# Conv tile 7's taps on TensorE for both chunks in two phases, and one more block of the first down projection by seven products

## The chip, the cores and the metric

The kernel runs on one core of one Trainium2 chip. The metric is the device time of one execution in microseconds, from the first to the last instruction with what lies around them. Besides the executions that are only timed, one execution was recorded by the hardware profiler; every view of the trace shown here is of that one.

A core has TensorE (PE in the profile, its weight loads as PEld), VectorE (DVE), ScalarE (ACT), GpSimd (POOL) and SyncE (SP, which here only issues DMAs). Each engine has its own instruction queue and works it off in order.

## The reference

Two layers over one sequence of 1024 tokens with 1024 channels, all in float32. Layer 0's mixer is the Conformer module, layer 1's a pooling mixer; each is followed by a SwiGLU feed-forward with F = 2816 hidden channels (22 F tiles of 128). Every sub-layer is RMS-normed, shifted, scaled and gated by a conditioning vector.

```python
# layer 0's mixer
u = h @ w1 + b1
a, g = jnp.split(u, 2, axis=-1)
u = a * jax.nn.sigmoid(g)
u = causal_depthwise_conv(u, w_dw, width=31) + b_dw     # one filter of 31 taps per channel
u = jax.nn.silu(layer_norm(u, ln_g, ln_b))
y = u @ w2 + b2
# layer 1's mixer: in four channel groups, trailing mean over 2, 4, 8, 16 tokens minus the token, then a linear map
# both layers' feed-forward
y = (silu(h @ w_gate) * (h @ w_up)) @ w_down
```

## The kernel before

**Layout.** Channels lie on the 128 partitions (8 tiles of channels), tokens along the free axis, in two chunks A and B of 512 tokens. TensorE's order is written out by hand: the program is a list of units, each a group of matmuls with the weights that it takes (`run_units`, up to five weight tiles `w` ahead, `W_BUFS`). Everything else is emitted between the units by `pace`, which steps background tasks as far as a running estimate of each engine's clock allows (`AHEAD`, `PRICES`, `DELAY`); the framework then orders the other engines' instructions.

**Products.** A product of two float32 tiles is three matmuls of 128x128 by 128x512 in the fp32r type (`products`): weight and activation are each split into a high part (ScalarE's cast) and a low part (value minus high part, VectorE as a rule), and high times high, high times low and low times high are summed in one PSUM bank.

**Conv taps.** The 31 taps of a channel tile are, for most tiles, scaled adds: VectorE adds `u * w` into a PSUM accumulator `ca`, ScalarE makes `pr = u * w` and GpSimd adds it into `pa`; class `Taps` hands each tap to whichever is free. Two tiles have taps on TensorE, where a tap is a matmul with a diagonal 128x128 weight (`PE_TAPS`, `pe_taps`): 15 taps of tile 6 and all 31 of tile 7, both for chunk A only. In chunk B all eight tiles go through VectorE and GpSimd. After chunk A's taps comes its layer norm (`layer_norm_silu`, task `ln_a`) beside three units of chunk B's `conv_in`, then `conv_out`. Chunk B's taps and layer norm (`ln_b`) run beside the first part of the feed-forward, and `conv_b` waits for it.

**Feed-forward of layer 0.** Gate and up projections are taken for F tiles in pairs `fp`. For `fp` 0 to 7 the even F tile of chunk A is computed classically and kept (`heads`), in two rounds of four, each followed by `down` of those four F tiles over all eight output tiles: 96 matmuls a round. The other gate and up products are done jointly for A and B by a scheme of seven products in place of eight (`all_joint`). The down projection is then finished in `first_down`. It has blocks `q` of two pairs (`q` = 5 has one), and each block has eight half products: odd or even F tile, chunk A or B, lower or upper half of the output channels; each is 24 matmuls (12 for `q` = 5). Blocks below `BEGINS[0] // 2` are classical, the others take seven products p1 to p7 with combined weights (s1 to s4) and combined activations (`kinds`, made in `paired` and kept in DRAM). Before, `q` = 0 to 3 are classical and `q` = 4, 5 (F tiles 16 to 21) go by seven. The order is: a and b (chunk A's odd tiles, both halves), p2, p1, p6, p7, p4, p5, p3, then c, d, e, f (chunk B). The weight sums s1, s2, s3 are made on VectorE in `weights`, from blocks a11, a21, a22 loaded ahead.

**Around it.** After p1 the pooling mixer of chunk A starts as a task on VectorE; its second half of x is whole only when p4 has ended; its output products (`pool_out`, tiles `mx`) come in `pool_end`, after e. `norm_a` of layer 1 then runs beside f.

Of the kernel before, what the change touches and what calls it, by code (L numbers as in the profile page):

```python
# [16 lines left out]
P = 128  # L17
D = 1024
# [35 lines left out]
DIAGS = 8  # L54
LOAD = {"load": 4.0, "both": 9.5, "slow": 6.0, "next": 4.0, "dots": 4.0}
# [5 lines left out]
BEGINS = (8, 0)  # L61
# [10 lines left out]
DELAY = {"stats": 2.75, "spread": 3.0, "soon": 0.5, "settled": 3.0, "later": 5.0, "root": 3.4}  # L72
# [4 lines left out]
for _name, _w in (  # L77
    ("ada_b", DEPTH * 6 * KT), ("norm_mix_g", DEPTH * KT), ("norm_ffn_g", DEPTH * KT),
    ("conv_b1", 2 * KT), ("conv_bdw", KT), ("conv_ln_g", KT), ("conv_ln_b", KT), ("conv_b2", KT),
    ("c", KT), ("pool_ls", KT), ("final_g", KT), ("conv_wdw", CW * KT),  # L80
):
    _COLS[_name] = _n
    _n += _w
# [18 lines left out]
def tap_groups(p):  # L102

    n = PE_TAPS[p]

    todo = list(range(CW - 1, -1, -1) if n == CW else range(CW - 3, CW - 3 - 2 * n, -2))
# [27 lines left out]
def trunk(ctx, tc, xT, c, vec, ada, adan, w1f, w1, wdg, w2, wgu, wdn, wds, wpl, out):  # L134
# [597 lines left out]
    def conv_u(ch, p):  # L732
        u = st["u", ch.i, p] = wslot(ch, "u", p)
        if ch.i == 0:
# [5 lines left out]
    def conv_glu(ch, p, ba, bg, own=False):  # L740
# [5 lines left out]
        if ch.i == 0 and PE_TAPS.get(p) == CW:  # L746

            V_.scalar_tensor_tensor(ba, ba, V("conv_b1", p), sg, op0=ADD, op1=MUL)
            pair = wpair(B, "us", F32R)
            hi, lo = st["us", p] = [pair[:, i, : ch.width] for i in range(2)]  # L750
            for part in (hi, lo):
                G_.memset(part[:, HALO - 2 : HALO].bitcast(F32), 0.0)
            S_.copy(hi[:, HALO:], ba)
            V_.tensor_tensor(lo[:, HALO:], ba, hi[:, HALO:].bitcast(F32), op=SUB)
            S_.copy(uhalo[:, p, :], ba[:, ch.n - HALO :])
            return
# [34 lines left out]

    def split_u(p):
# [6 lines left out]
    def pe_taps(p):  # L799
# [4 lines left out]
        for i, js in enumerate(groups):  # L804
            def emit(take, i=i, js=js):
# [3 lines left out]
                for q, j in enumerate(js):  # L809
                    full = PE_TAPS[p] == CW  # L810
                    o = (CW - 1 - j) // 2 * 2 if full else CW - 3 - j
                    c = j + o if full else 0
                    products(b[:, o:], wt, q, [v[:, c : c + A.n - o] for v in st["us", p]], j == groups[0][0], j == groups[-1][-1])
                    if q % 4 == 3:
                        pace()
                if i == len(groups) - 1:
                    if full:
                        S_.activation(st["u", 0, p][:, HALO:], b, AF.Identity, bias=V("conv_bdw", p))
                        st["taps", 0][p] = True
                    else:  # L820
                        T["taps", 0, p].other = b
# [86 lines left out]
    def layer_norm_silu(ch):  # L908
# [17 lines left out]
        yield "soon" if ch.i else "stats"  # L926
# [51 lines left out]
    def conv_out(ch, squares, then=None):  # L978
# [17 lines left out]
        for ds in [(0, 1) if ch.i else (0,), *(() if ch.i else ((1,),)), *((d,) for d in range(2, KT))]:  # L996
# [475 lines left out]
    def down(ch, l, fs, then=()):  # L1472

        def half(d0, wd):
            def kept(take, give):
                gs = [st["g", ch.i, f] for f in fs]
                last = len(gs) - 1
                todo = [range(4)] if not d0 else [range(2), range(2, 4)]
                for ds in todo:
                    bs = {d: bank("dn") for d in ds}  # L1480
                    for i, g in enumerate(gs):
# [6 lines left out]
                        if ds is todo[-1] and d0:  # L1488
# [164 lines left out]
    def first_down(l, after):  # L1653

        SIDE = {"odd": 0, "even": 1}
        duo, one = BY_SEVEN[l]
        todo, raw, banks, ready, counts = [], {duo: {}, one: {}}, {}, {}, [0, 0]
# [10 lines left out]
        def fetched_raw(name, b):  # L1668
            for q in (one, duo):
# [3 lines left out]
        def first_blocks():  # L1673
            wide = [block("u0", "raw", F32).rearrange("p a b -> p (a b)") for _ in range(2)]
            both = block("u0", "raw", F32)
            raw[duo].update(a11=wide[0], a22=wide[1])
            raw[one].update(a11=both[:, 0], a22=both[:, 1])
            fetched_raw("a11", 0)
            fetched_raw("a22", 3)

        def second_blocks():
            a21, a21_one = (block("h1", "a21", F32).rearrange("p a b -> p (a b)") for _ in range(2))
            raw[duo]["a21"], raw[one]["a21"] = a21, a21_one[:, : duo_width(one) * 512]
# [573 lines left out]
```

## Time and profile before

| | |
|---|---|
| median of 3 runs | 1677.97 us (1677.6 to 1678.09) |
| the profiled execution | 1675.66 us |
| its span, first to last instruction | 1673.9 us |
| mean granted TensorE clock | 0.998 |
| matmuls | 7550 |
| PE busy | 1651.8 us, 99% |
| DVE busy | 1310.0 us, 78% |
| ACT busy | 804.1 us, 48% |
| POOL busy | 487.4 us, 29% |

The profiled execution was 2.3 us shorter than the median of the timed ones, and 1.76 us of it lie outside the span. In rows of the profile `out<-in` gives the tiles that an instruction writes and reads, `xN` how many instructions a row joins, and what stands in brackets the idle time before it and who ended that. All kernel calls go through helpers, so nearly all compute rows have line L128 or L151; tiles tell them apart. Matmuls are pipelined, so the time that one takes in a stream is the spacing of starts, not the duration of one: the chain of waits shows it, since it counts each from the end of the one before.

### The profile page before, as it was taken

To read this page: it belongs to the slowest core of one execution; us is meant where nothing else is said; L and a number is where in the kernel's file an instruction comes from. 1 tells how busy PE (TensorE), PEld (TensorE's weight loads), DVE (VectorE), ACT (ScalarE), POOL (GpSimd) and SP (SyncE) were. 2 spreads that over 40 slices of the span, in tenths; PEclk is the share of its full clock that TensorE was granted. 3 is DMA by queue.
4 is the path that set the end of the run, shared out by engine and by line. 5 is a ranking of instruction groups with operands and counts; after the bars stand their busy time and mean duration, and the time that the engine had idled before them with its cause. 6 is when DMAs were issued, how large, how long until landed. Compare 5 with 4: busy or idle time off the path is not lost.

```text
span 1673.9 us, 21194 instructions
## 1 busy us (share of the span) xinstructions
PE 1651.8 (99%) x7550; PEld 1351.2 (81%) x7550; DVE 1310.0 (78%) x1867; ACT 804.1 (48%) x1090; POOL 487.4 (29%) x567
## 2 busy tenths in 40 slices
PE   7999999999999999999999999999999999999997
PEld 5777878787888888888888888888888888888887
DVE  8889899799759888888678957848777766658657
ACT  3669696867546332332234436637322222244354
POOL 3587777796002111221100502101111111000013
PEclk9999999999999999999999999999999999999999
DMA  8958997828776888886965959866777776686664
GB/s 301 295 176 228 225 236 205 226 78 241 229 234 168 278 264 287 282 272 206 400 231 164 285 155 283 247 211 199 189 225 222 220 227 183 207 273 207 192 170 126
DMA packets 117180, 378.60 MB, mean 226 GB/s; under 512 B 12369, under 2 KB 14545, under 8 KB 117074
## 3 DMA queue, kind: packets, MB, share of 16 engines
q1 hardware_dynamic: 79664, 245.63, 41.6%
q0 software_dynamic: 36832, 131.09, 32.5%
q8 instruction: 59, 0.97, 0.2%
q10 hardware_dynamic: 578, 0.53, 0.1%
q14 instruction: 47, 0.39, 0.1%
HBM read 310.61 MB, written 62.39 MB: 223 GB/s over the span
## 4 chain that ended last, share of the span: by engine, by line
PE 88%; POOL 3%; DVE 2%; DMA 2%; issue 2%; ACT 2%; DVEq 0%; SPq 0%; POOLq 0%; ACTq 0%
PE a L151 24%; PE dn L151 23%; PE e L151 14%; PE p L151 10%; PE y L151 6%; POOL pa L128 3%; PE first L151 3%; PE g L151 2%; PE tap L151 2%; DMA adaw<-in_adan_dram 1%; DMA s<-in_wds_dram 1%; PE ada L151 1%; ACT w L128 1%; DMA w<-in_wgu_dram 1%; PE var L151 1%
## 5 line engine op out<-in xcount | busy, mean ns | idle before, releaser
L128 ACT CAST w<-raw 128x1024 fp32r<-128x1024 f32 (+1 forms) x247 | 254.6, 1033 | 305.5 <-PE dn L151 56.9
L128 DVE TENSOR_TENSOR w<-raw,w 128x1024 fp32r<-128x1024 f32 (+1 forms) x173 | 209.3, 1214 | 62.2 <-ACT w L128 61.9
L151 PE MATMUL a<-n,w 128*128 128x512 f32 x1056 | 246.8, 389 | 0.2
L151 PE MATMUL p<-h,w 128*128 128x512 f32 x1056 | 243.7, 390 | 1.2 <-DMA w<-in_wgu_dram 1.0
L128 POOL TENSOR_TENSOR pa<-pa,pr 128x512 f32<-128x512 f32 x159 | 225.3, 1500 | 29.0 <-ACT pr L128 23.7
L151 PEld LDWEIGHTS p<-h,w 128*128 128x128 f32 x1056 | 197.3, 188 | 43.7 <-DMA w<-in_wgu_dram 1.4
L151 PEld LDWEIGHTS a<-n,w 128*128 128x128 f32 x1056 | 198.0, 188 | 42.2 <-DVE r L128 1.1
L151 PE MATMUL dn<-hi,w 128*128 128x512 f32 (+1 forms) x768 | 226.2, 377 | 0.4 <-DVE w L128 0.4
L151 PE MATMUL dn<-g,w 128*128 128x512 f32 x864 | 199.1, 390 | 0.2 <-DVE x L128 0.2
L151 PEld LDWEIGHTS dn<-g,w 128*128 128x128 f32 x864 | 161.7, 188 | 34.7 <-DVE x L128 0.6
L128 DVE SCALAR_TENSOR_TENSOR ca<-u,vecs,ca 128x512 f32<-128x512 f32 x246 | 170.6, 747 | 0.5
L151 PEld LDWEIGHTS dn<-hi,w 128*128 128x128 f32 x768 | 141.2, 188 | 27.0 <-DVE w L128 0.9
L151 PE MATMUL dn<-lo,w 128*128 128x512 f32 (+1 forms) x384 | 144.3, 376 | 0.0
L151 PE MATMUL a<-t,w 128*128 128x512 f32 x528 | 123.3, 389 | 0.0
L151 PE MATMUL e<-t,w 128*128 128x512 f32 x528 | 123.3, 389 | 0.0
L151 PE MATMUL e<-b,w 128*128 128x512 f32 x528 | 123.3, 389 | 0.0
L128 ACT ACTIVATE pr<-u,vecs 128x512 f32<-128x512 f32 x159 | 108.4, 717 | 25.0 <-POOL pa L128 19.7
L151 PEld LDWEIGHTS a<-t,w 128*128 128x128 f32 x528 | 99.1, 188 | 20.7
L151 PEld LDWEIGHTS e<-t,w 128*128 128x128 f32 x528 | 99.1, 188 | 20.6
L151 PEld LDWEIGHTS e<-b,w 128*128 128x128 f32 x528 | 99.1, 188 | 20.6
L1191 POOL DMA_DIRECT2D raw<-in_wgu_dram x41 | 36.5, 889 | 271.5 <-DVE r L128 104.2
L128 ACT CAST hi<-op 128x1024 fp32r<-128x1024 f32 (+1 forms) x52 | 48.5, 935 | 87.1 <-PE dn L151 77.2
(191 smaller groups left out, 2449.4 us busy)
## 6 DMA issues: line engine op xcount, KB each, us to landing
raw<-in_wgu_dram SPq DMA_DIRECT2D x132, 512.0 KB, 4.7
raw<-in_wds_dram SPq DMA_DIRECT2D x48, 512.0 KB, 6.0
adaw<-in_ada_dram POOLq DMA_DIRECT2D x48, 512.0 KB, 6.8
kinds<-k POOLq DMA_DIRECT2D x42, 512.0 KB, 7.7
raw<-in_wgu_dram POOLq DMA_DIRECT2D x41, 512.0 KB, 7.3
raw<-in_w_dram SPq DMA_DIRECT2D x36, 512.0 KB, 6.6
op<-kinds SPq DMA_DIRECT2D x36, 512.0 KB, 4.8
adaw<-in_adan_dram SPq DMA_DIRECT2D x32, 512.0 KB, 5.5
```

The costliest lines, as they stand in the source:

```text
L128: self.last = self.order(getattr(self.eng, name)(out, *args, **kw))
L151: last_mm[0] = nc.tensor.matmul(out, lhsT, rhs, start=start, stop=stop, skip_group_check=more).ins.name
L1191: d = order(nc.gpsimd.dma_start(w[i], wgu[l, fp, src], accum_op=ADD))
```

## The change

1. **Tile 7's taps.** Both chunks of tile 7 are now done on TensorE, as two groups of 64 channels. `halves` writes the gated value so that partitions 0 to 63 hold the even tokens and 64 to 127 the odd tokens of 64 channels; a dense 128x128 weight then does two taps for both phases at once, and a group takes 16 steps (`NM`) over 512 columns, which cover 1024 tokens. That is 2 groups x 16 steps x 3 = 96 matmuls (`pe_halves`) in place of 31 taps x 3 = 93 of 482 to 512 columns. VectorE does four gated multiplies of 64 x 256 a chunk in place of one of 128 x 512, and ScalarE writes the result back in four pieces of 64 x 256 a group. Tile 7 of chunk B no longer goes through VectorE and GpSimd.
2. **Block q = 3 by seven products.** `BEGINS` goes from 8 to 6, so F tiles 12 to 21 (`q` = 3, 4, 5) go by seven. In `heads` the second round's `down` leaves out F tiles 12 and 14 for the upper half; for the lower half they stand for that block's p2. c and d now cover `q` = 0, 1, and e and f only `q` = 2; `pool_end(A)` comes after d.
3. **Weight sums on GpSimd.** s1, s2 and s3 are made on GpSimd; a22 is loaded when it is needed, twice, and a11 and a21 are loaded as blocks of their own.
4. **Order.** The matmul for chunk A's mean is put 4.6 instead of 2.75 into the estimate (`DELAY["mean"]`), and chunk A's first two output tiles in `conv_out` share a unit, as chunk B's did.

```diff
-BEGINS = (8, 0)
+BEGINS = (6, 0)
...
+    def halves(ch, p, ba, sg):
+        n = ch.n // 2
+        t = temp(ch.n).rearrange("p (g n) -> p g n", g=2)
+        for g in range(2):
+            at = slice(HALF * g, HALF * g + HALF)
+            for f in range(2):
+                V_.scalar_tensor_tensor(t[HALF * f : HALF * f + HALF, g], ba[at].rearrange("p (n f) -> p f n", f=2)[:, f], V("conv_b1", p)[at],
+                                        sg[at].rearrange("p (n f) -> p f n", f=2)[:, f], op0=ADD, op1=MUL)
...
+        hi, lo = (part[:, :, LEAD + ch.i * n : LEAD + ch.i * n + n] for part in st["us", p])
+        S_.copy(hi, t)
+        V_.tensor_tensor(lo, t, hi.bitcast(F32), op=SUB)
+
+    def pe_halves(p):
+        blocks = [(g, m) for g in range(2) for m in range(NM)]
...
+                    products(b, wt, q, [part[:, g, m : m + 512] for part in st["us", p]], m == 0, m == NM - 1)
...
+                    if m == NM - 1:
+                        for ch in chunks:
+                            n = ch.n // 2
+                            d = st["u", ch.i, p][HALF * g : HALF * g + HALF, HALO:].rearrange("p (n f) -> p f n", f=2)
+                            for f in range(2):
+                                at = slice(HALF * f, HALF * f + HALF)
+                                S_.activation(d[:, f], b[at, n * ch.i : n * ch.i + n], AF.Identity, bias=V("bdw_halves", g)[at])
...
-        yield "soon" if ch.i else "stats"
+        yield "soon" if ch.i else "mean"
...
-        for ds in [(0, 1) if ch.i else (0,), *(() if ch.i else ((1,),)), *((d,) for d in range(2, KT))]:
+        for ds in [(0, 1), *((d,) for d in range(2, KT))]:
...
-                gs = [st["g", ch.i, f] for f in fs]
+                gs = [st["g", ch.i, f] for f in fs if not d0 or f // 2 < BEGINS[l]]
...
             if kind == "s2":
-                mine["s1"] = block("h1", "s1", F32).rearrange("p a b -> p (a b)")[:, :n]
-                order(V_.tensor_tensor(mine["s1"], mine["a21"], mine["a22"], op=ADD))
-                tc.add_manual_dep(V_.last.ins, last_mm[0], edge, reason="behind the products")
-                V_.tensor_tensor(mine["a21"], mine["a11"], mine["a21"], op=SUB)
-                V_.tensor_tensor(mine["a11"], mine["a11"], mine["s1"], op=SUB)
+                mine["s1"] = wide("h1", "s1", q)
+                order(G_.tensor_tensor(mine["s1"], mine["a21"], mine["a22"], op=ADD))
+                tc.add_manual_dep(G_.last.ins, last_mm[0], edge, reason="behind the products")
+                G_.tensor_tensor(mine["a21"], mine["a11"], mine["a21"], op=SUB)
+                G_.tensor_tensor(mine["a11"], mine["a11"], mine["s1"], op=SUB)
...
+            mine = [q for q in qs if kind != "a12" or q >= ROUNDS[l] * ROUND // 2]
...
-        for qs, names in ((range(duo // 2), "cd"), (range(duo // 2, duo), "ef")):
+        for some_qs, names in ((range(2), "cd"), (range(2, begins), "ef")):
...
-    taps(B, *some, *rest[: len(rest) - HOLD - HOLD_LN])
+    taps(B, *[p for p in some if PE_TAPS.get(p, 0) < CW], *rest[: len(rest) - HOLD - HOLD_LN])
...
-        "e": lambda: pool_end(A),
+        "d": lambda: pool_end(A),
```

More of the change, by code (lines that the diff above doesn't have):

```diff
@@ L104, in tap_groups @@
     n = PE_TAPS[p]
-    todo = list(range(CW - 1, -1, -1) if n == CW else range(CW - 3, CW - 3 - 2 * n, -2))
+    todo = list(range(CW - 3, CW - 3 - 2 * n, -2))
     return [todo[i : i + DIAGS] for i in range(0, len(todo), DIAGS)]
@@ L745, in conv_glu @@
             tc.add_manual_dep(S_.last.ins, st.pop("v_high"), edge, reason="behind the layer norm's last high part")
[L746 to L755, printed above, removed]
+        if PE_TAPS.get(p) == CW:
+            halves(ch, p, ba, sg)
             return
@@ L809, in emit @@
                 for q, j in enumerate(js):
[L810 to L813, printed above, removed]
+                    o = CW - 3 - j
+                    products(b[:, o:], wt, q, [v[:, : A.n - o] for v in st["us", p]], j == groups[0][0], j == groups[-1][-1])
                     if q % 4 == 3:
@@ L816, in emit @@
                 if i == len(groups) - 1:
[L817 to L821, printed above, removed]
+                    T["taps", 0, p].other = b
             us.append((emit, wdg[sum(len(tap_groups(q)) for q in PE_TAPS if q < p) + i]))
@@ L1655, in first_down @@
         SIDE = {"odd": 0, "even": 1}
-        duo, one = BY_SEVEN[l]
-        todo, raw, banks, ready, counts = [], {duo: {}, one: {}}, {}, {}, [0, 0]
+        qs = list(BY_SEVEN[l])[::-1]
+        begins = BEGINS[l] // 2
+        raw, banks, ready, counts = {q: {} for q in qs}, {}, {}, [0, 0]
         steps = []
@@ L1688, in weights @@
             mine = raw[q]
-            if kind in ("a12", "s4"):
-                mine[kind] = raws.tile([P, D], F32, tag="raw", name=nm("raw"))[:, :n]
-                nc.sync.dma_start(mine[kind], wds[l, q, 1][:, :n])
+            at_once = {"a12": 1, "s4": 1, "a22": 3, "s2": 3}.get(kind)
+            if at_once is not None:
+                mine["a22" if kind == "s2" else kind] = r = raws.tile([P, D], F32, tag="raw", name=nm("raw"))[:, :n]
+                nc.sync.dma_start(r, wds[l, q, at_once][:, :n])
                 if kind == "s4":
@@ L1708, in seven @@
         def seven(name, kind, of, key, fresh, ends):
-            for q in (one, duo):
-                steps.append((name, key, fresh and q == one, q == duo, ends, lambda q=q: weights(kind, q), operand(l, of, q)))
-        classical(A, range(duo), 0, ("odd",), "a")
-        classical(A, range(duo), 1, ("odd",), "b")
+            mine = [q for q in qs if kind != "a12" or q >= ROUNDS[l] * ROUND // 2]
+            for q in mine:
+                steps.append((name, key, fresh and q == mine[0], q == mine[-1], ends, lambda q=q: weights(kind, q), operand(l, of, q)))
+        classical(A, range(begins), 0, ("odd",), "a")
+        classical(A, range(begins), 1, ("odd",), "b")
         seven("p2", "a12", "b21", "y", True, [(A, 0)])
@@ L2022, in trunk @@
     for p in PE_TAPS:
-        for u in pe_taps(p):
+        for u in pe_halves(p) if PE_TAPS[p] == CW else pe_taps(p):
             unit(*u)
@@ L2224 @@
             diag[i, range(P), q, range(P)] = taps[j, p]
+    dense = np.zeros((len(whole), 2, NM, 2, HALF, 2, HALF), np.float32)
+    for i, p in enumerate(whole):
+        for m in range(NM):
+            for f in range(2):
+                for o in range(2):
+                    j = 2 * (m - LEAD) + CW - 1 + f - o
+                    if 0 <= j < CW:
+                        dense[i, :, m, f, range(HALF), o, range(HALF)] = taps[j, p].reshape(2, HALF).T
+    dense = dense.reshape(-1, DIAGS, P, P).transpose(0, 2, 1, 3)
+    diag = np.concatenate([diag, dense])
     down = np.asarray(ffn_w_down).reshape(DEPTH, NP, 2, P, 2, D // 2)
```

70 lines of the change are left out of this document (43 added, 27 removed).

## The prediction

> **What bounds the kernel now.** I read the page first, then who TensorE waits for.
>
> ```profile
> span 1673.9 us, 21194 instructions
> PE 1651.8 (99%) x7550; PEld 1351.2 (81%) x7550; DVE 1310.0 (78%) x1867; ACT 804.1 (48%) x1090; POOL 487.4 (29%) x567
> ```
>
> ```profile
> PE var L151 <- DVE acc L128: 4.9, 1, 4.9
> PE c L151 <- DMA crow<-in_c_dram: 2.9, 1, 2.9
> PE rstd L151 <- DVE col L128: 1.9, 1, 1.9
> PE rstd L159 <- DVE col L128: 1.7, 1, 1.7
> PE first L151 <- ACT h L128: 1.6, 1, 1.6
> PE p L151 <- DMA w<-in_wgu_dram: 1.0, 1, 1.0
> PE dn L151 <- DVE w L128: 0.4, 1, 0.4
> PE ada L151 <- DMA adaw<-in_adan_dram: 0.3, 1, 0.3
> ...
> PE dn L151 <- DVE x L128: 0.2, 1, 0.2
> PE p L151 <- ACT r L128: 0.2, 1, 0.2
> ```
>
> TensorE is the bound: 99% busy. The five longest waits, 13.0 us, belong to the first norm at the start and the last one at the end, which the change leaves alone. What waits between is small: 1.0 + 0.3 + 0.2 + 0.2 = 1.7 us, the most of it for a weight. So the kernel is as long as its list of matmuls, and a change pays by taking matmuls away without opening a wait. What one costs in the stream is read from the chain of waits (start, us, what, count).
>
> ```profile
> 167.38 5.69 PE tap L151 x24
> 181.66 18.47 PE tap L151 x81
> 450.08 43.52 PE y L151 x192
> 816.35 93.84 PE dn L151 x414
> ```
>
> Both 93.84 / 414 and 43.52 / 192 give 0.2267 us a matmul of 512 columns. A tap costs 18.47 / 81 = 0.228 us with about 500 columns, and 5.69 / 24 = 0.237 us in the first group, whose first step comes behind other work.
>
> **The seven products: what goes.** Before, block 3 is eight half products of 24 matmuls, 192. After, it is seven, 168: p2 (chunk A's even tiles, lower half) stays in the second `down` of the heads, the other six stand in `first_down`. So 24 matmuls go: 24 x 0.2267 = **-5.44 us**. The Trainium skill's page TensorE: Matmul & The Clock Gate (Back-to-back issue gap) puts a matmul of N columns at N / 2.4 + 2.5 ns, 216 ns here, by which the same 24 would be worth 5.2 us; the trace has 227 ns and decides.
>
> Where they go matters. In `first_down` a and b lose 48, c to f 96, and p1 and p3 to p7 gain 144: zero. All 24 leave the heads' second `down`, and behind that stands chunk B's layer norm:
>
> ```profile
> 416.66 1.10 PE L151 MATMUL mean<-acc,ones 128*128 128x512 f32 x2
> 417.19 14.19 PE L151 MATMUL dn<-g,w 128*128 128x512 f32 x60
> 449.92 10.36 PE L151 MATMUL y<-v,w 128*128 128x512 f32 x45
> ```
>
> ```profile
> 415.83 0.69 DVE L128 TENSOR_TENSOR acc<-acc,u 128x512 f32<-128x512 f32 x1
> 450.12 2.50 DVE L128 TENSOR_TENSOR v<-t,v 128x512 fp32r<-128x512 f32 x4 [1.92 <-ACT v L128]
> ```
>
> The mean's matmul starts right after VectorE's last sum (415.83 + 0.69), and `y` starts while the last four `v` are still being made. The norm takes the 33.3 us from mean to `y` and has no slack: take 5.44 us of matmuls from between and TensorE waits 5.44 us, unless the mean comes that much earlier. That is what the other part must pay for.
>
> **Tile 7's taps.** TensorE: 96 matmuls of 512 columns for 93 narrower ones. Before, 93 x 0.228 = 21.2 us. After, between 96 x 0.2267 = 21.8 and 96 x 0.237 = 22.8; I take the middle, 22.3: **+1.1 us** (+0.6 to +1.6). The new operand starts at odd columns too, but so does the old one (each second tap reads from column 29 on), at 0.228 us. For VectorE and GpSimd:
>
> ```profile
> L128 DVE SCALAR_TENSOR_TENSOR ca<-u,vecs,ca 128x512 f32<-128x512 f32 x246 | 170.6, 747 | 0.5
> L128 POOL TENSOR_TENSOR pa<-pa,pr 128x512 f32<-128x512 f32 x159 | 225.3, 1500 | 29.0 <-ACT pr L128 23.7
> ```
>
> ```profile
> 379.32 11.93 DVE L128 SCALAR_TENSOR_TENSOR ca<-u,vecs,ca 128x512 f32<-128x512 f32 x18
> ```
>
> Chunk B loses a tile of 30 taps. Shared 246 to 159 as now, 18 leave VectorE and 12 GpSimd; 18 take 11.93 us in a run. So the last sum can come some 12 us earlier, and 5.44 are needed: I cost the shorter cover at nothing, and a tap relief under 5.44 us costs the difference. What is late next is the heads' weights, as now.
>
> What `halves` adds, by the nearest rows:
>
> ```profile
> L128 DVE SCALAR_TENSOR_TENSOR x<-dn,gains,x 128x256 f32<-128x256 f32 x8 | 3.8, 479 | 1.2 <-PE dn L151 1.0
> L128 ACT COPY t<-ada 128x256 f32<-128x256 f32 x4 | 1.4, 358 | 0.0
> L128 ACT ACTIVATE u<-tap,vecs 128x512 f32<-128x512 f32 x1 | 0.7, 689 | 1.4 <-PE tap L151 1.4
> ```
>
> VectorE: eight multiplies of 256 elements, 8 x 0.48 = 3.8 us, and one low part more (0.7), for two of 0.75: +3.0 us, ahead of chunk A's layer norm. ScalarE: four writes behind the last tap, 4 x 0.36 = 1.4 us where one took 0.69. Chunk A's norm is also just in time, so 3.0 us could show as a wait at the first `y`, which starts while the last `v` are being made:
>
> ```profile
> 238.91 11.58 PE L151 MATMUL y<-v,w 128*128 128x512 f32 x48
> ```
>
> ```profile
> 241.92 0.69 DVE L128 TENSOR_TENSOR v<-t,v 128x512 fp32r<-128x512 f32 x1 [1.11 <-ACT v L128]
> ```
>
> Against it stand the taps' own 1.1 us, and the joint unit of `conv_out`: with 48 matmuls in place of 24 the eighth `v` is needed 7 x 3 x 0.2267 = 4.8 us later. The later mean takes 1.85 us of that. 1.1 + 4.8 - 1.85 - 3.0 = 1 us of slack: nothing, within a microsecond. The short waits around the mean and first `y` may go; with the 1.0 us for a weight, behind GpSimd's taps, I take **-0.5 us** for waits between 0 and -1.7.
>
> **The sums on GpSimd.** Nine adds, in units of 512 elements 15 (one for each of block 5's three, two for the others').
>
> ```profile
> 281.78 3.80 POOL L128 TENSOR_TENSOR pa<-pa,pr 128x512 f32<-128x512 f32 x3 [1.45 <-ACT pr L128]
> 361.61 13.00 POOL L128 TENSOR_TENSOR pa<-pa,pr 128x512 f32<-128x512 f32 x9
> ```
>
> ```profile
> L128 POOL TENSOR_TENSOR w<-raw,w 128x1024 fp32r<-128x1024 f32 x6 | 20.5, 3425 | 27.5 <-ACT w L128 27.5
> ```
>
> ```profile
> 840.00:880.00 40.00, 40.00 (x178) 33.14 (x177) 28.91 (x38) 13.66 (x19) 0.53 (x1) 1.00 0.64 226
> ```
>
> The last row is a stretch of 40 us: its fifth pair is GpSimd's, 0.53 us. It is idle there, so nothing stands ahead of the sums. They cost 15 x 1.27 = 19.0 us (three in 3.80), 21.7 (nine in 13.00) or 25.7 (3.425 for 1024). The time for them: weights are asked for five steps ahead, so the first sums at the end of p2's first step; the last must be done for p6's third step. Between lie 24 (p2) + 60 (p1) + 36 (p6) = 120 matmuls, 27.2 us, less the cast and the low part:
>
> ```profile
> 417.03 1.22 DVE L128 TENSOR_TENSOR w<-raw,w 128x1024 fp32r<-128x1024 f32 x1
> 371.34 2.12 DVE L128 TENSOR_TENSOR w<-raw,w 128x1024 fp32r<-128x1024 f32 x1 [0.19 <-ACT w L128]
> ```
>
> ```profile
> L128 ACT CAST w<-raw 128x1024 fp32r<-128x1024 f32 x238 | 249.0, 1049 | 286.4 <-DMA raw<-in_wgu_dram 54.6 <-PE e L151 51.5 <-PE dn L151 46.6
> ```
>
> 27.2 - 1.05 - 1.22 = 24.9 us. I take 21.7, the row of GpSimd beside a VectorE at work: done with 3 us to spare, cost nothing. Behind a waiting sum stand GpSimd's DMA issues for the conditioning weights, which nothing in this stretch waits for.
>
> **What else moves in `first_down`.** VectorE gives up three sums each for blocks 5 and 4 (5.7 us) and, for block 3, four classical low parts (4.9); it gets six weight and six operand low parts (14.6) and one s4 (1.2): +5 us, in a stage where it is busy 28.9 of 40 us. In the joint part pairs 6 and 7 cost VectorE one instruction of 0.69 us more each and ScalarE three less; GpSimd issues one 256 KB write more a pair, SP one load. a22 is loaded twice, 2.5 MB in all, by SP, a few units ahead of need. The mixer of chunk A: p4 ends 48 matmuls (10.9 us) later, while `pool_out` stays at the same place, 732 matmuls in.
>
> ```profile
> 964.30 0.68 DVE L128 TENSOR_TENSOR mx<-win,mx 128x512 fp32r<-128x512 f32 x1
> ```
>
> ```profile
> 983.63 10.88 PE y L151 x48
> ```
>
> Its last value has 18.7 us to spare now; less 10.9, less VectorE's 5: 3 us. Nothing, but thin. `norm_a` keeps its cover, 96 matmuls of e and f in place of f's 96.
>
> **Sum.** -5.44 + 1.1 - 0.5 = -4.8 us. On the profiled execution: span 1673.9 to 1669.1, time 1675.66 to 1670.9. On the median, 2.3 us above that execution: 1677.97 to **1673.2 us**. A measurement can tell 0.2%, 3.4 us, from no change.
>
> **Rivals.** *A: the sums collide with VectorE.* The same low part took 1.22 us alone and 2.12 us while GpSimd added (13.00 us from 361.61 on). In the 24.9 us stand about eight low parts of 1.22 us, 9.8 us. If none of them overlaps GpSimd's adds, 19.0 + 9.8 = 28.8 us: p6's third step waits 3.9 us, and the change is worth -0.9, 1677.1 us. For it: the 2.12. Against: nine in 13.00 us were taken beside a busy VectorE. Chance 0.10. The Trainium skill's page SBUF — State Buffer (Who interferes with whom) states the rule: a VectorE instruction with two SBUF inputs and a GpSimd one that reads SBUF block each other fully. The two rows agree.
>
> *B, slower: the same at GpSimd's dear rate.* At 3.425 us for 1024, 25.7 + 9.8 = 35.5 us, 10.6 late: +5.8, 1683.8 us. It decides against the change when the sums take over 24.9 + 4.8 = 29.7 us, and measurably from 33.1. For it: it is the one row of GpSimd with 1024 elements. Against: that one writes fp32r. Chance 0.07.
>
> *C: chunk B's norm does not come earlier.* The order estimate could hand out the freed time to other work: up to +5.4, 1678.6. For it: no slack now; against: 12 us freed. Chance 0.08.
>
> *D: the mixer misses `pool_out`.* 3 us of slack gone and 3 more: 1676.2. Chance 0.07.
>
> *E: the dense taps do not do what they should:* if operands of the two-phase form stream at half speed, 96 x 0.2267 = 21.8 us more, 1695. Nothing in the tap rows shows it. Chance 0.04.
>
> **How the numbers follow.** Forecast 0.64, its own range 1670.2 (waits gone, taps at the cheap end, and a microsecond of spread) to 1674.6. Cases A, C and D lie within 0.2%, 0.25; B and E are slower, 0.11; faster 0.64. To leave out no more than 0.2, the range goes up past D and A to 1677.5, and leaves out B, C, E.
>
> **What would show it.** 7529 matmuls (7550 - 24 + 3); the taps' 96 in 22 us; VectorE's last `acc` and the mean before the second `down` has begun or early in it, and no wait before `y`; s1 to s3 as GpSimd rows of 1.3 and 2.5 to 2.9 us; no wait at p6 or `pool_out`. A `dn` that waits for `w` near p6 shows A or B; a `y` of chunk B that waits for `v` shows C; a `y` that waits for `mx` shows D. The forecast is wrong if new waits of TensorE add up to over 1.4 us.

## The result, and the profile after

The changed kernel took 1703.5 us in the median of four runs (1702.3 to 1708.7) against 1678.0 for the kernel before on the same chip: a ratio of 1.0156 (95% interval 1.0133 to 1.0179). It is 25.5 us slower; the forecast was 4.8 us faster. The profiled execution took 1702.42 us, 26.8 more than that of before. The head of its page:

```profile
span 1700.6 us, 21152 instructions
PE 1656.3 (97%) x7529; PEld 1351.8 (79%) x7529; DVE 1322.9 (78%) x1859; ACT 800.5 (47%) x1084; POOL 488.4 (29%) x562
```

The list of matmuls is as short as forecast, 7529. But PE's share fell from 99% to 97%: TensorE stands idle more. (It is also "busy" 4.5 us longer with 21 matmuls fewer: the mean granted clock is 0.994 in place of 0.998. What pulls it down is read in the last section.) Who it waits for, by the view of the waits for PE:

```profile
PE var L153 <- DVE acc L130: 6.0, 1, 6.0
PE dn L153 <- DVE x L130: 5.6, 7, 1.5
PE y L153 <- ACT t L130: 4.6, 1, 4.6
PE p L153 <- ACT r L130: 3.6, 2, 3.4
PE mean L153 <- DVE acc L130: 3.0, 1, 3.0
PE c L153 <- DMA crow<-in_c_dram: 2.9, 1, 2.9
PE a L153 <- ACT t L130: 2.2, 2, 1.1
...
PE ada L153 <- DMA adaw<-in_adan_dram: 1.5, 2, 1.1
```

Five kinds are new or grown: `dn` for VectorE's reads of the banks, `y` for `t`, `p` for `r`, `mean` for `acc`, `a` for `t`. With 1.2 more for `ada` (the matmuls for the conditioning vector) they make 20 us. Lines L153 and L130 are L151 and L128 of before. Nearly all of it can be placed by setting the two traces side by side at the starts of certain matmuls. Each row is a stretch up to the start named; the columns behind "before" are differences from it in us. The kernels named `a_` to `d_` are the experiments below.

| up to the first | before | after | a_seven | a_taps_order | a_order | c_taps_fixed | d_hold | d_taps_hold | d_nosums |
|---|---|---|---|---|---|---|---|---|---|
| `a` of channel tile 4, chunk A | 65.8 | +1.4 | +0.6 | +0.5 | +0.1 | +0.3 | +1.2 | +0.5 | +0.7 |
| `tap` | 101.5 | +5.2 | +0.8 | +4.7 | +2.3 | +5.0 | +2.8 | +3.5 | +2.8 |
| matmul behind the taps | 32.7 | +1.2 | 0.0 | +1.2 | 0.0 | +1.2 | +1.2 | +1.2 | +1.2 |
| chunk A's `mean` | 5.5 | +3.2 | 0.0 | +3.2 | 0.0 | +0.5 | +3.6 | +0.5 | +3.6 |
| chunk A's `y` | 33.5 | +1.7 | 0.0 | +1.7 | 0.0 | +0.1 | +0.1 | +0.1 | +1.7 |
| `dn` of the heads | 107.5 | +6.8 | 0.0 | +6.1 | +5.6 | +0.2 | +6.1 | +0.1 | +6.4 |
| chunk B's `y` | 103.5 | -2.3 | -3.2 | +7.4 | +4.6 | +6.7 | -6.0 | +0.5 | -0.2 |
| joint product | 66.6 | 0.0 | +10.2 | 0.0 | 0.0 | 0.0 | +1.5 | +0.8 | 0.0 |
| chunk A's `pool_out` | 466.9 | +8.0 | +8.4 | 0.0 | 0.0 | 0.0 | +11.5 | 0.0 | +2.6 |
| the end | 690.5 | +1.6 | +0.8 | +0.5 | 0.0 | +0.4 | +0.5 | +0.4 | +0.8 |
| span | 1673.9 | +26.8 | +17.6 | +25.4 | +12.6 | +14.4 | +22.4 | +7.8 | +19.6 |

Three things have to be known to read it. The second row also moves in kernels whose code up to there is that of before (a_seven +0.8, a_order +2.3): the matmuls for `ada` meet a load that is sometimes late. And before's profiled execution lies 2.3 us below its median, so differences of profiled executions come out some 0.5 to 2.7 us larger than those of medians (5.5 in c_seven_fixed). And the same code does not give the same stretch once there are waits in it. In five kernels with the changed kernel's code in the down (after, b_single, b_gbank, c_spill, d_hold) the row of `pool_out` lies 7.8 to 11.5 over before; and three kernels that differ from the changed one only behind it (b_sumsv, b_s4dma, d_nosums) have -0.1, -0.1 and -0.2 in the row of chunk B's `y`, where the changed kernel has -2.3.

**Chunk A's first `y`.** Chronological rows of TensorE and of ScalarE of the changed kernel (start, us, what, count, and in brackets the idle time before it and who ended that):

```profile
251.57 0.98 PE L153 MATMUL y<-v,w 128*128 128x512 f32 x3
257.13 8.06 PE L153 MATMUL y<-v,w 128*128 128x512 f32 x24 [4.58 <-ACT t L130]
```

```profile
253.62 0.80 ACT L130 ACTIVATE t<-u,vecs 128x512 f32<-128x512 f32 x1
254.46 0.62 ACT L130 CAST v<-t 128x512 fp32r<-128x512 f32 x1
255.09 1.28 ACT L130 ACT_TABLE_LOAD   x1
256.39 0.69 ACT L130 ACTIVATE t<-g,vecs 128x512 f32<-128x512 f32 x1
```

The unit with two output tiles opens a second bank after three matmuls. That bank is still `g` of the `conv_in` just ahead, and its reader, the sigmoid (`t<-g`), stands in ScalarE's queue behind the norm's last silu and a table load of 1.28 us. Behind the wait, 24 matmuls take 8.06 us, 0.336 each on average in place of 0.227.

**`p` ahead of chunk B's `conv_out`**, by the same two views:

```profile
461.50 5.73 PE L153 MATMUL p<-h,w 128*128 128x512 f32 x24 [3.38 <-ACT r L130]
```

```profile
459.92 1.04 ACT L130 CAST w<-raw 128x1024 fp32r<-128x1024 f32 x1 [4.65 <-DMA raw<-in_w_dram]
460.87 1.07 ACT L130 COPY r<-p 128x512 f32<-128x512 f32 x2
```

ScalarE works in order: the copy that empties `p`'s banks stands behind the cast of a `conv_out` weight whose load is late.

**`first_down`.** Rows of GpSimd and of VectorE in the same 20 us, then TensorE:

```profile
877.25 2.42 POOL L130 TENSOR_TENSOR s<-a,raw 128x1024 f32<-128x1024 f32 x1
879.62 2.40 POOL L130 TENSOR_TENSOR a<-a,s 128x1024 f32<-128x1024 f32 x1
881.97 2.40 POOL L130 TENSOR_TENSOR a<-a,a 128x1024 f32<-128x1024 f32 x1
```

```profile
871.54 2.91 DVE L130 TENSOR_TENSOR w<-a,w 128x512 fp32r<-128x512 f32 x1
...
878.15 7.91 DVE L130 TENSOR_TENSOR lo<-op,hi 128x512 fp32r<-128x512 f32 x2
...
889.44 2.05 DVE L130 SCALAR_TENSOR_TENSOR x<-dn,gains,x 128x512 f32<-128x512 f32 x3
```

```profile
890.33 0.47 PE L153 MATMUL dn<-hi,w 128*128 128x512 f32 x1 [1.48 <-DVE x L130]
```

The row of 7.91 us joins two low parts. One, of 512 columns, took 6.78 where the other 13 of its size take 0.67 to 0.69; the second, of 1024, took its usual 1.21. The first ran while GpSimd made three sums in a row, until 884.4. Just before it, three low parts of weights (`w<-a,w` at 861.9, 867.3 and 871.5) were longer too, by 0.3, 0.8 and 2.2: 9.4 us of VectorE in all, and none such in b_sumsv or d_nosums, where GpSimd makes no sums. The reads of the finished banks (`x<-dn`) stand behind in VectorE's queue, and the next product adds into the same banks, so TensorE waits for the read. Of the seven waits, three come right behind the long low parts (0.58 at 877.0, 1.48 at 890.3, 0.41 at 893.0), and two behind the additions for s4 (`raw<-raw,a`), before which VectorE stands for a load (1.12 at 908.0, 1.06 at 921.0). VectorE and TensorE at the first of these two:

```profile
906.63 0.69 DVE L130 TENSOR_TENSOR raw<-raw,a 128x512 f32<-128x512 f32 x1 [1.64 <-DMA raw<-in_wds_dram]
907.24 0.74 DVE L130 SCALAR_TENSOR_TENSOR x<-dn,gains,x 128x512 f32<-128x512 f32 x1
```

```profile
908.04 0.50 PE L153 MATMUL dn<-hi,w 128*128 128x512 f32 x1 [1.12 <-DVE x L130]
```

The last two (0.63 and 0.30 from 950.4 on) have counterparts in kernels without sums on GpSimd (0.63 and 0.96 in b_sumsv).

### The profile page after: what moved, and what is told of

Same layout as the page of the kernel before. It is cut to its first block, busy times and chain, and to the rows that moved or that the text cites. A ratio compares the mean times of both kernels' runs of the same rounds, so it can differ in the third digit from the quotient of the medians.

```text
span 1700.6 us, 21152 instructions
## 1 busy us (share of the span) xinstructions
PE 1656.3 (97%) x7529; PEld 1351.8 (79%) x7529; DVE 1322.9 (78%) x1859; ACT 800.5 (47%) x1084; POOL 488.4 (29%) x562
## 5 line engine op out<-in xcount | busy, mean ns | idle before, releaser
L130 ACT CAST w<-raw 128x1024 fp32r<-128x1024 f32 (+1 forms) x239 | 246.7, 1035 | 283.2 <-DMA raw<-in_wgu_dram 61.7
L153 PE MATMUL dn<-hi,w 128*128 128x512 f32 (+1 forms) x864 | 257.7, 379 | 6.4 <-DVE x L130 5.6
L153 PE MATMUL p<-h,w 128*128 128x512 f32 x1056 | 244.4, 391 | 4.8 <-ACT r L130 3.6
L153 PE MATMUL a<-n,w 128*128 128x512 f32 x1056 | 246.8, 389 | 0.2
L130 DVE TENSOR_TENSOR w<-raw,w 128x1024 fp32r<-128x1024 f32 (+1 forms) x167 | 201.2, 1210 | 44.4 <-ACT w L130 44.4
L153 PEld LDWEIGHTS p<-h,w 128*128 128x128 f32 x1056 | 197.3, 188 | 47.4 <-ACT r L130 4.5
L153 PEld LDWEIGHTS a<-n,w 128*128 128x128 f32 x1056 | 198.0, 188 | 42.2 <-DVE r L130 1.1
L130 POOL TENSOR_TENSOR pa<-pa,pr 128x512 f32<-128x512 f32 x148 | 211.5, 1505 | 32.1 <-ACT pr L130 29.5
L153 PEld LDWEIGHTS dn<-hi,w 128*128 128x128 f32 x864 | 159.2, 188 | 39.6 <-DVE x L130 4.1
L153 PE MATMUL dn<-lo,w 128*128 128x512 f32 (+1 forms) x432 | 163.1, 378 | 0.0
L153 PE MATMUL dn<-g,w 128*128 128x512 f32 x696 | 159.9, 390 | 0.1
L130 DVE SCALAR_TENSOR_TENSOR ca<-u,vecs,ca 128x512 f32<-128x512 f32 x229 | 159.1, 747 | 0.7
L153 PEld LDWEIGHTS dn<-g,w 128*128 128x128 f32 x696 | 130.3, 188 | 27.4 <-DVE x L130 0.5
L153 PE MATMUL a<-t,w 128*128 128x512 f32 x528 | 123.3, 389 | 0.0
L153 PE MATMUL e<-b,w 128*128 128x512 f32 x528 | 123.2, 389 | 0.0
L153 PE MATMUL e<-t,w 128*128 128x512 f32 x528 | 123.2, 389 | 0.0
L130 ACT ACTIVATE pr<-u,vecs 128x512 f32<-128x512 f32 x148 | 101.2, 716 | 35.3 <-POOL pa L130 25.8
L153 PEld LDWEIGHTS a<-t,w 128*128 128x128 f32 x528 | 99.1, 188 | 20.6
L153 PEld LDWEIGHTS e<-t,w 128*128 128x128 f32 x528 | 99.1, 188 | 20.6
L153 PEld LDWEIGHTS e<-b,w 128*128 128x128 f32 x528 | 99.1, 188 | 20.6
L130 ACT CAST hi<-op 128x1024 fp32r<-128x1024 f32 (+1 forms) x58 | 55.0, 948 | 109.6 <-PE dn L153 100.9
```

Of the source, the lines that this page charges most:

```text
L130: self.last = self.order(getattr(self.eng, name)(out, *args, **kw))
L153: last_mm[0] = nc.tensor.matmul(out, lhsT, rhs, start=start, stop=stop, skip_group_check=more).ins.name
```

## The experiments

Each group of runs was on another chip, with the kernel before run beside it: its medians were 1678.2, 1676.7, 1677.6 and 1678.9 for the groups `a_` to `d_`, and the ratio in brackets is to that one. The changed kernel was run only beside the first before, 1678.0. So what a run is said to differ from the changed kernel is taken between chips, and a us or two of it can be the chip; what an edit did is read from the stretches of the traces.

**Each part alone** (`a_seven`, `a_taps_order`, `a_taps`, `a_order`). The diff of the change is taken in three pieces: the seven products with their sums; tile 7's taps; and the two order edits (the pair of tiles in `conv_out`, the longer delay of the mean).

> Before, with the seven products for F tiles 12 to 21 and their sums on GpSimd alone; taps and the two order edits stay as before. Theory (each part loses at its own place, and the losses add up): the 24 products leave the heads' second down, -5.4; the first layer's down loses 8.0 to TensorE's waits for VectorE's reads x<-dn at the changes of product; the 3.4 wait at p behind the second down may come or not. So +2.6 to +6.0, 1680.6 to 1684. Rival (the two parts disturb each other: the down is late only because the taps part shifted the work around it): the prediction's own term stands, -4.8, 1673.2.

Measured: 1693.4, 15.2 over before (ratio 1.0089, 1.0062 to 1.0116): slower than either had it. The down lost 8.4 without any help from the taps. What neither had is chunk B's `y`, in the view of the waits and in the windows of 10 us around it (PE's busy time comes first behind the length, and behind POOL's pair stand the granted clock, the DMA engines' share and GB/s):

```profile
PE y L151 <- DVE v L128: 5.0, 2, 2.5
PE y L151 <- ACT v L128: 3.5, 1, 3.5
```

```profile
442.00:452.00 10.00, 4.09 (x19) 3.00 (x18) 7.58 (x13) 6.60 (x11) 0.00 (x0) 0.73 0.94 362
452.00:462.00 10.00, 10.00 (x35) 8.02 (x34) 3.70 (x6) 5.05 (x8) 2.32 (x3) 0.76 0.92 226
```

The 24 matmuls are gone, and TensorE waits 8.5 us for `v` in their place, with a clock of 0.73 to 0.76 around the waits: together +7.0 over the two rows of the table. Without the tap relief the shorter `down` is worse than worth nothing.

> Before, with channel tile 7's taps as two phases for both chunks and the two order edits (two tiles of conv_out in one unit for chunk A, the longer delay of its mean); down as before. Theory (losses add up): the conv stage of chunk A loses 18 to 20 against before, 1.1 of it the three more products: 1696 to 1698, and p of the feed forward starts about 20 later than before. Rival (the parts disturb each other): the taps part alone costs its three products, 1679.

Measured: 1701.2, 22.9 over before (1.0135, 1.0113 to 1.0158). Chunk A's conv stage lost about what the theory said (the first six rows: 17.4), and 7.4 more went ahead of chunk B's `y`, again at `p` behind `r` (5.3 of wait). So the rival is out, and the theory left one place out. The parts do interact there and only there in any size: alone +7.0 and +7.4, together -2.3.

> Before, with channel tile 7's taps as two phases for both chunks, without the two order edits. Theory (losses add up): y of chunk A no longer loses the 6.9 that the changed kernel lost between its first and last y, as the pair of tiles doesn't ask for a second bank while the sigmoid holds it; the rest of the loss stays: +11 to +13, 1689 to 1691. Rival (the order edits are the whole loss): +1.1, 1679.

Measured: 1706.6, 28.4 over before (1.0167, 1.0144 to 1.0191). The pair's loss went, as the theory has it (the stretch up to the heads' `dn` +2.7 in place of +6.1). But without the longer delay the mean waits 5.8 for `acc` instead of 3.0, the stretch from it to `y` gives up another 3.0, and the one ahead of chunk B's `y` loses 10.8. The delay is needed by this part; the pair is not.

> Before, with the two order edits alone: conv_out takes its first two tiles in one unit for chunk A as well, and chunk A's mean gets the longer delay. Theory (the pair needs a second bank, which the conv_in ahead of it holds until the sigmoid, which ScalarE does behind the norm's silus and a table load): TensorE waits about 4 to 5 for ACT t at the second y, with 1.4 to 2 of slower clock behind it: +5 to +7, 1683 to 1685. Rival (the wait is there only since the two-phase taps make the norm late): within 1 of before, 1678.

Measured: 1688.2, 10.0 over before (1.0059, 1.0037 to 1.0081), above both. The theory's wait is there, 4.06 at the second `y`, and its stretch costs +5.6, so the pair needs no late norm to lose. Another 4.6 went ahead of chunk B's `y`, which it didn't have: there the mean waits 3.0 for `acc` and `p` 1.6 for `r`.

**One repair each** (`b_single`, `b_gbank`, `b_sumsv`, `b_s4dma`), on the changed kernel. Over the kernel before on their own chip the four lie at +23.4, +22.3, +27.2 and +25.1, where the changed kernel has +25.5; their intervals overlap with its interval, so the times alone don't part them from it.

```diff
-        for ds in [(0, 1), *((d,) for d in range(2, KT))]:
+        for ds in [(0, 1) if ch.i else (0,), *(() if ch.i else ((1,),)), *((d,) for d in range(2, KT))]:
```

> The changed kernel with one tile of conv_out in each unit for chunk A again (the longer delay of its mean stays). Theory (the pair asks for a second bank while the sigmoid's tile of the conv_in ahead still holds it): the wait of 4.6 for ACT t at the second y goes, with the 1.4 to 2 of slower clock behind it: -6 to -7, 1696.5 to 1697.5. Rival (the wait only moves: the norm of chunk A's v comes late anyway, and single units wait for it or the end of the stage takes it back): within 2 of the changed kernel, 1702 to 1704.

Measured: 1700.1 (1.0138, 1.0123 to 1.0153), 3.4 less than the changed kernel. The wait at the second `y` is gone, and its stretch falls from +6.8 to +0.5, as the theory has it. Ahead of chunk B's `y` it has +1.7 where the changed kernel has -2.3, and in the down 1.7 more. Against the three kernels with the changed kernel's code up to there, at -0.1 and -0.2, 1.8 of the 4.0 remain; the 1.7 in the down are within what equal code showed. The theory holds for its stretch; how much is given back by the rival's mechanism is not settled.

```diff
-        t = temp(ch.n).rearrange("p (g n) -> p g n", g=2)
+        t = bg.rearrange("p (g n) -> p g n", g=2)
```

(`bg` is the bank of `g`, which is handed to `halves`.)

> The changed kernel with the product of the halves written into the bank of g instead of an SBUF tile, so that the low part reads one operand from PSUM. Theory (two operands in SBUF are held up while GpSimd works): the two low parts take about 0.7 each instead of 3.7, chunk A's sums end up to 6 earlier, and the wait of 3.0 at the mean goes with the slower clock behind it: -3 to -4.5, about 1699.5. Rival (GpSimd's or ScalarE's chain for the taps ends the sums, not VectorE's time): the low parts are short and the mean waits the same, 1703.

Measured: 1699.0 (1.0133, 1.0116 to 1.0150), -4.5. The low part of the halves, by the view of the tile `us`, in the changed kernel and in this one (count, then min, median and max in ns):

```profile
L130 DVE TENSOR_TENSOR us<-t,us x2: 3512/3711/3910, 133.2 to 164.0; 128x512 fp32r<-128x512 f32 x2
```

```profile
L130 DVE TENSOR_TENSOR us<-g,us x2: 684/688/692, 141.2 to 160.0; 128x512 fp32r<-128x512 f32 x2
```

The same subtraction takes 3.7 us with two operands in SBUF beside a GpSimd at work on the taps, and 0.69 with one of them in PSUM. (Of the two in the second kernel, the one at 160.0 ran beside two adds of GpSimd; at the other GpSimd stood idle.) The two stretches around the mean fall from +3.2 and +1.7 to +0.5 and +0.1. The theory is confirmed; the price is that `a` now waits 2.8 once, for VectorE's reading of the bank of `g`.

```diff
-                order(G_.tensor_tensor(mine["s1"], mine["a21"], mine["a22"], op=ADD))
+                order(V_.tensor_tensor(mine["s1"], mine["a21"], mine["a22"], op=ADD))
```

(and the two lines of s3 and s2 in the same way)

> The changed kernel with the sums of the seven products (s1, s2, s3) on VectorE instead of GpSimd; GpSimd is then nearly idle there. Theory (GpSimd's sums hold up VectorE's operations on two SBUF operands by some 11 to 12 in this stage, so that the reads of the banks come late): VectorE gets 8 to 9 of sums to do and loses the 11 to 12 of hold-ups, the down stage keeps half or less of its 8: -3 to -6, 1697.5 to 1700.5. Rival (VectorE is late by the amount of its work and by the loads of s4's tiles): the same or worse, 1703 to 1708.

Measured: 1703.9 (1.0160, 1.0145 to 1.0175), +0.4 on the changed kernel. In the down itself the theory is right: +4.7 in place of +8.0, although VectorE does nine sums more, and under the 7.8 to 11.5 of equal code. The view of the tile `op` shows why, in the changed kernel and in this one:

```profile
L130 DVE TENSOR_TENSOR lo<-op,hi x58: 674/1219/6778, 827.0 to 1670.1; 128x1024 fp32r<-128x1024 f32 x44, 128x512 fp32r<-128x512 f32 x14
```

```profile
L130 DVE TENSOR_TENSOR lo<-op,hi x58: 681/1222/1227, 827.2 to 1671.2; 128x1024 fp32r<-128x1024 f32 x44, 128x512 fp32r<-128x512 f32 x14
```

With GpSimd adding, one low part of 512 took 6.78 us; without, the longest of that size takes 0.69, and the longest of all 58, of 1024 columns, 1.23. What was won went again in the next layer, where the order of VectorE's work came out another way:

```profile
1058.08 1.15 PE L153 MATMUL var<-ones,acc 128*128 128x1 f32 x8 [2.00 <-DVE acc L130]
```

One wait of 2.0, with a granted clock of 0.96 over the 40 us around it: 3.9 us lost.

```diff
-                if kind == "s4":
-                    V_.tensor_tensor(mine["s4"], mine["s4"], mine["s2"], op=ADD)
...
+            if kind == "a22":
+                mine["s4"] = mine["s2"]
+                order(nc.gpsimd.dma_start(mine["s4"], wds[l, q, 1][:, :n], accum_op=ADD))
```

> The changed kernel with s4 formed by a transfer that adds a12 onto s2's tile, instead of a load through the ring of three tiles and an addition on VectorE. Theory (VectorE stands behind s4's late loads, and the reads of the banks behind it): the waits at the changes of product after 900 us go, about 3 of the stage's 8: -2 to -4, 1699.5 to 1701.5. Rival (hold-ups by GpSimd make all of them): within 1, 1703.

Measured: 1701.8 (1.0150, 1.0134 to 1.0165), 1.7 under the changed kernel, and set against the before of its own chip no different from it. The trace bears the mechanism out. In the changed kernel VectorE stood 1.64 us for s4's load at 906.6, and 3.07 and 0.65 before the additions at 915.3 and 918.3 (for the 3.07 the profile names no cause), with `x<-dn` behind them; TensorE's two waits behind that, 2.2 us at 908.0 and 921.0, are gone. But the two from 950.4 on grew from 0.9 to 2.0. The stretch is +6.3, where equal code without the edit has 7.8 to 11.5: a gain is likely, and its size is not shown.

**The wait at `p`, and repairs together** (`c_spill`, `c_all`, `c_taps_fixed`, `c_seven_fixed`).

```diff
-            x_out(A)
+            for m in range(KT // 2):
+                d = nc.sync.dma_start(xd[0][m], xp[0][m])
+                tc.add_manual_dep(d.ins, last_mm[0], edge, reason="behind the first unit")
```

> The changed kernel with the store of chunk A's x (four tiles of 512 KB) put behind the first unit of chunk B's conv_out instead of ahead of it. Theory (the store meets the loads of conv_out's weights, ScalarE stands in its queue for such a load, and the copy of p behind it keeps TensorE): the wait of 3.4 at p and what slower clock follows it go from the stretch between the heads' second down and conv_out: -3 to -5, 1698.5 to 1700.5. Rival (the loads of conv_out's weights are late by themselves, since their tiles come free late): the wait stays, within 1 of the changed kernel.

Measured: 1703.2 (1.0152, 1.0132 to 1.0171). The store now goes out at 469 and the wait at `p` is still there, 4.2. The theory is out: the store is not what delays these loads.

> The changed kernel with single tiles in chunk A's conv_out, the halves' product in the bank of g, the sums on VectorE, s4 by an adding transfer, and the store of chunk A's x behind conv_out's first unit. Theory (waits with places of their own, so that what is won at each stays): -6.4 and -4.5 in chunk A's conv stage, -3 to -5 ahead of chunk B's conv_out, -4 to -5 in the first layer's down: -18 to -21, 1682.5 to 1685.5. Rival (what is won ahead of chunk B's norm is given back there, as the single tiles gave back 3 to 4 and the bank 2): -12 to -15, 1688.5 to 1691.5.

Measured: 1693.5 (1.0089, 1.0074 to 1.0104), -10: less than either. The conv stage kept its repairs; ahead of chunk B's `y` it is 1.4 over before with 3.5 of wait at `p`; the sums on VectorE cost their 3.9 in the next layer again, behind the same wait of 2.0 at `var`.

> Before, with channel tile 7's taps as two phases for both chunks, the longer delay of the mean, single tiles in conv_out and the halves' product in the bank of g; down as before. Theory (the two repairs are worth in this kernel what they were worth in the changed one): the taps part with the order edits, 1701.2, less 6.4 and 4.5: 1689 to 1691; chunk A's conv stage then costs 6 to 8 more than before, and the rest is lost ahead of chunk B's conv_out. Rival (the repairs overlap, both being the slower clock behind the same waits): 1693 to 1696.

Measured: 1690.2 (1.0073, 1.0058 to 1.0088), as the theory has it. Its stretch ahead of chunk B's `y` loses 6.7, and its chronological rows show the chain. SP's issues first (`raw<-in_wgu` are weights of the first joint tile, `raw<-in_w` those of `conv_out`), then ScalarE and TensorE:

```profile
429.94 0.33 SPq L1131 DMA_DIRECT2D raw<-in_wgu_dram  x1
...
431.86 0.33 SPq L1131 DMA_DIRECT2D raw<-in_wgu_dram  x1
...
435.05 0.33 SPq L1131 DMA_DIRECT2D raw<-in_wgu_dram  x1
...
437.46 0.33 SPq L1131 DMA_DIRECT2D raw<-in_wgu_dram  x1
...
449.84 0.81 SPq L498 DMA_DIRECT2D raw<-in_w_dram  x2
```

```profile
457.81 1.04 ACT L130 CAST w<-raw 128x1024 fp32r<-128x1024 f32 x1 [7.63 <-DMA raw<-in_w_dram]
458.76 0.58 ACT L130 COPY r<-p 128x512 f32<-128x512 f32 x1
```

```profile
459.39 4.61 PE L153 MATMUL p<-h,w 128*128 128x512 f32 x12 [4.40 <-ACT r L130]
```

Chunk B's norm is early, so the buffers of its `u` come free early, and the joint tile's four loads, which take those buffers, go out at 430 to 437, over 90 us ahead of their use. `conv_out`'s next weights follow at 450 and land too late. In the kernel before the four go out later, at 440 to 450, and five of `conv_out`'s weights have gone ahead of them.

> Before, with the seven products for F tiles 12 to 21 alone, the sums on VectorE and s4 by an adding transfer. Theory (two losses: chunk B's norm, which the shorter down no longer hides, and VectorE's late reads in the down): the down stage loses 3 to 4 less, the 10 at chunk B's conv_out stay: 1688.5 to 1690.5. Rival (the stage's loss is the products' order and not VectorE's load): 1692.5 to 1694.

Measured: 1691.3 (1.0079, 1.0058 to 1.0100), between the two and nearer to the theory. The down loses 3.4 in place of 8.4, better than the theory's size, and the loss at chunk B's `y` stays, as it says; the sums on VectorE then cost 5.5 in the next layer.

**The last two open points** (`d_hold`, `d_taps_hold`, `d_all`, `d_nosums`).

```diff
                 w[i] = quarter(l, fp, i, "u1")
+                if l == 0 and fp == 0:
+                    tc.add_manual_dep(quarter.last, st["first_y"], edge, reason="behind the first unit")
```

(`first_y` is the last matmul of chunk B's first `conv_out` unit, `quarter.last` the load just issued.)

> The changed kernel with the four loads of the first joint tile's gate and up weights held behind the first unit of chunk B's conv_out. Theory (chunk B's norm comes early, its buffers come free early, and these loads of 2 MB go out ahead of conv_out's own weights, for which ScalarE and then TensorE wait at p): the wait of 3.4 goes and the stretch up to conv_out keeps the whole 5.44 of the products left out: -3 to -4, 1699.5 to 1700.5. Rival (conv_out's weights are late because their own tiles come free late): the wait stays, 1703.

Measured: 1700.4 (1.0132, 1.0115 to 1.0149), -3.1. The wait at `p` is gone:

```profile
PE p L153 <- ACT r L130: 0.3, 1, 0.3
```

The stretch ahead of chunk B's `y` is 6.0 shorter than before, more than the 5.44 of the products, and 1.5 of it goes at a late weight in `y`. This is the theory's cause. The down came out 3.5 longer than in the changed kernel, on the same code: there TensorE waits 7.4 us for `x<-dn` in place of 5.6, and behind one of the two waits more, 1.45 at 963.6, the granted clock is 0.79 over 8 us.

> The repaired taps part alone (two phases, longer delay of the mean, single tiles, product in the bank of g) with the same four loads held. Theory (early loads of the joint tile): the 6.7 that its stretch up to chunk B's conv_out loses against before go: 1690.2 less 6 to 7, 1683 to 1684.5, and chunk A's conv stage with its three products is what is left. Rival: 1690.

Measured: 1686.0 (1.0040, 1.0025 to 1.0055), 1.5 over the range; 6.2 of the 6.7 went, as the theory has it.

> The changed kernel with single tiles in chunk A's conv_out, the product in the bank of g, s4 by an adding transfer (sums on GpSimd) and the four loads held. Theory: the stretch up to chunk B's conv_out gains 5.44 against before, chunk A's conv stage up to its taps costs 5, the taps 1.2, the down 6.3, ends and start 1 to 2: 1685 to 1688, so the change as a whole doesn't reach before even so. Rival (the norm of chunk B is again the bound once the loads are away): 1690 to 1693.

Measured: 1688.2 (1.0060, 1.0045 to 1.0075), 0.2 over the theory's range: the heads' stretch gained 5.0, and the down cost 9.2 where 6.3 was put.

> The changed kernel with the sums of the seven products left out (s1, s2 and s3 take a21 and a11 as they are, s4 takes a12 alone; the products are all done, on other numbers). Theory (GpSimd's hold-ups of VectorE and s4's additions make most of the down stage's 8): the stage loses 0 to 2 against before: -6 to -8, 1695.5 to 1697.5. Rival (the products' number and order, three q in a row on the same banks, make it): the stage keeps over half, 1699.5 or more.

Measured: 1697.0 (1.0109, 1.0094 to 1.0124), -6.5. With the sums left out the down loses 2.6 in place of 8.0, and VectorE's reads cost one wait:

```profile
PE dn L153 <- DVE x L130: 0.7, 1, 0.7
```

Another 1.3 is waited for a late weight. So 5.4 of the 8.0 are the sums, s4's included (5.2 to 8.9 against the 7.8 to 11.5 of equal code); the products' number and order keep at most 2.6, and that rest was not taken apart. No version here beat the kernel before; the nearest, d_taps_hold, is 0.4% slower and has three matmuls more than it.

## Why the prediction was wrong, step by step

The list of matmuls came out as forecast. What failed is that the prediction kept TensorE the bound and put every new wait at nothing. By size: `first_down` with its sums, put at nothing, cost 8.0, of which 5.4 go with the sums (d_nosums); the joint unit of `conv_out`, put at 4.8 of slack, cost 6.8; what `halves` adds, put at nothing, cost 4.9; and of the -5.44 at the heads only 2.3 came.

**"24 matmuls go, -5.44": right in the list, not in the time.** The prediction said that chunk B's norm has no slack and that the other part must bring the mean earlier. Both hold: alone, the shorter `down` costs 7.0 (a_seven); with the taps the mean comes 24.5 us earlier against the start of the heads' `dn` (70.3 behind it before, 45.8 after), where 12 was put. What failed is the sentence behind it, that what is late next is the heads' weights as now. It was `conv_out`'s weights: an earlier norm frees buffers, the joint tile's loads take them, and 3.4 are waited at `p`. d_hold holds these loads back, and the stretch keeps 6.0. Of the 5.44, the changed kernel has 2.3, and even these are likely luck of the one profiled execution: the three kernels with the same code up to there wait 3.8 to 3.9 at this `p` in place of 3.4, the granted clock falls to 0.79 over 8 us behind it, which it did not do here, and they keep 0.1 to 0.2.

**"Tile 7's taps, +1.1": right**, +1.2 in each run that has them.

**"`halves` adds 3.0 us to VectorE, against 1 us of slack: nothing": a row mis-sized.** The eight multiplies were right (3.9 us measured for 3.8). The low part was priced at 0.7, which is what the one of before took (0.68, with one operand in PSUM); the new one has both in SBUF beside GpSimd's taps, and two took 7.4 (b_gbank: 0.69 each). The mean waits 3.0, and its two stretches lose 4.9.

**"The joint unit of `conv_out` gives 4.8 us of slack": the wrong sign.** It was counted as time for the eighth `v`; that it needs a second bank, and who holds it, was not asked. Its stretch loses 5.6 to 6.8 wherever it is in (a_order has it alone) and 0.1 to 0.5 in the repaired kernels without it (b_single first).

**"-0.5 for waits".** (The 1.7 us of small waits that it is taken from leave out the row of 0.4 for `dn` behind `w`; that changes nothing.) The short waits around the mean didn't go, they grew; ahead of the taps 5.2 came on top. Up to 3.4 of that also shows in kernels that change nothing there (+3.4 in c_seven_fixed), so only the rest can be put down to the taps, likely by the two waits of 1.1 at `a` for the sigmoid; no run tried that alone.

**"The sums cost nothing, 21.7 us of 24.9": right for GpSimd, wrong for whom it stops.** GpSimd's sums took 20.2 us and no weight was late for p6: rivals A and B fell in the place that they named. Their mechanism, GpSimd and VectorE holding each other up, worked all the same, in the other direction: four of VectorE's low parts take 9.4 us more, one of them 6.78 in place of 0.68, and VectorE's reads of the banks, which the prediction left out, keep TensorE. Together with s4's additions behind late loads this is what d_nosums takes away, 5.4; how it is shared between the two, and the remaining 2.6, stay open. The Trainium skill's page SBUF — State Buffer (Who interferes with whom) has a VectorE instruction with two SBUF inputs contend with a GpSimd one that reads SBUF. The rows agree: 6.78 beside GpSimd's sums, at most 0.69 without. The "+5 us" for VectorE in a stage with room went to nothing on paper because the room was read as an average.

**Rivals C, D, E.** C's wait happened in a_seven, where there is no tap relief, at 7.0 where 5.4 was the most; in the whole change the norm is in time. D didn't: no wait at `pool_out`. E didn't.

**Sum.** Forecast -5.44 + 1.1 - 0.5. By the profiled executions: -2.3 at the heads, +1.2 taps, +4.9 around the mean, +6.8 at the joint unit, +8.0 in the down, +5.2 ahead of the taps, +3.0 at the two ends: 26.8. The prediction's own mark for being wrong, over 1.4 us of new waits, was passed by each of five.

## What to carry to other kernels

Taking matmuls off a saturated TensorE pays only if everything that was timed against them gets earlier too, and what gets earlier frees buffers and sends loads ahead of more urgent ones: ask for each freed buffer who takes it. For each instruction moved to GpSimd, or newly with two SBUF operands, price the partner that it stops and what stands behind that in its queue, above all the reads that free PSUM banks. A unit that opens two banks at once must be checked for who still holds the second one.

## What the runs showed of the hardware that was not expected

**A short wait costs more than its length.** Behind 4.58 us of waiting, 24 matmuls took 8.06 us, 2.6 more than at 0.227 each: the first eleven started 0.43 apart, the rest 0.23. Behind 2.0 us at `var`, 1.9 more were lost. A window shows the clock granted around the first, 0.91 over 40 us:

```profile
240.00:280.00 40.00, 35.42 (x167) 27.34 (x166) 36.87 (x54) 30.30 (x41) 25.62 (x23) 0.91 0.70 192
```

It does not always come: behind the 3.38 us at 461.5, 24 matmuls took 5.73, which is 0.239 each. Over all 18 traces, from 30 to 1600 us, each of the 21 waits of TensorE of 3.47 us or more has a granted clock of 0.79 or less over the 8 us behind it; of the 25 between 2.0 and 3.43 us 20 have 0.81 or less and five 1.00; of the 68 between 1 and 2 us only five have 0.80 or less. What decides it among the shorter ones was not tried.

**How far GpSimd stretches a VectorE operation.** In one kernel the same subtraction of 512 columns took from 0.67 to 6.78 us; the longest lasted over three of GpSimd's sums, which followed each other without a gap, and ended some 0.6 us behind the last.
